# One level of Strassen's product in the up projection of a convolutional feed-forward, with all gated tiles through DRAM

## The chip, the core and the metric

The kernel runs on one core of a Trainium2 chip. The metric is the device time of one execution in microseconds (us). TensorE (PE) multiplies, with its weight loads shown apart as PEld; VectorE (DVE), ScalarE (ACT) and GpSimd (POOL) do the elementwise work; SyncE (SP) issues the DMAs of this kernel.

## The reference, cut to what matters

One layer of an encoder over 1024 prompt frames and 8 x 16 sample frames, 1152 tokens in all, D_MODEL = 1024 and D_FF = 2816. Attention, a state-space layer and the output projection come first and are the same before and after the change. Then:

```python
def conv_ffn(x, prev, w_up, conv_w, conv_b, w_down):
    up = x @ w_up                                   # [tokens, 2 * D_FF]
    up_p = jnp.concatenate([prev, up], axis=1)      # two earlier rows
    c = sum(up_p[:, j:j + L] * conv_w[j] for j in range(CONV_W)) + conv_b
    gate, val = jnp.split(c, 2, axis=-1)
    return (jax.nn.silu(gate) * val) @ w_down, up_p[:, -(CONV_W - 1):]
...
    f, new_conv = conv_ffn(rmsnorm(x, lw['norm2']), conv_prev, ...)
    x = x + f                                       # then a final rmsnorm
```

## The kernel before

Every product runs in float32r with each operand split into a high and a low part, so `mm3` (L60 to L63) issues three matmuls for one: high by high, high by low, low by high. Tokens are cut into 9 tiles of 128 (8 of the prompt, 1 of the sample).

`wout_s(t)` finishes the output projection of tile t: two halves of 512 columns, 12 matmuls each, into `po`; DVE adds the residual; the rows go to `x2_d` in DRAM; ACT squares them, `rstd` makes the norm on DVE in small pieces, ACT scales the rows. `h2_T(t)` (L1210 to L1213) transposes the scaled rows on PE into `h2T`, ACT copies them into `h2h` and DVE subtracts into `h2l`, 128x512 at a time.

The up projection runs over 22 pairs j, each of one tile of 128 gate features (i = 0) and one of 128 value features (i = 1). `load_up(j, i)` brings 8 blocks of `w_up` and splits them with the norm's gain into `uh` and `ul` (8 ACT and 8 DVE instructions of 128x128). For each of three token blocks of 384, `up_mm` runs 8 x 3 matmuls into a bank `pu`; `up_out` copies the bank to `ext` on ACT. So a pair has 2 x 3 x 8 x 3 = 144 matmuls of 384 columns.

`up_pair_end(j)` then does the convolution over time of both tiles (`up_conv`: one Identity on ACT, L1301, and two DVE instructions, L1302 and L1303, all 128x1168), Silu on ACT (L1308) and the product on DVE. POOL fills the two leading columns of `ext` (L1292, L1293) and saves the last rows (L1299, L1300). Of the gated tiles `g`, the first five (KEEP) stay in SBUF; the other 17 go to `g_d` in DRAM and are reloaded as `gr` (L1346) for the down projection.

The down projection runs over two token halves (5 and 4 tiles) by two halves of 512 output columns; for each it goes over k = 0 to 21, with `down_k` splitting a piece of `w_down` (`wd` into `wdh`, `wdl`) and of the gated tile (into `gh`, `gl`), and 3 matmuls of 512 columns per token tile into `acc`. The pool `dwA` that holds these pieces is opened ahead of the up projection, so that the first pieces are there when it ends. `conv_out` writes the saved convolution rows (`cvo`, `cvr`) while the down projection runs.

The order of the work on each engine is set by a scheduler that replays the program on its own timeline; within an engine the order is then fixed, and engines wait for each other on semaphores.

## Time and profile before

| | us |
|---|---|
| three timed runs | 1271.71, 1274.02, 1273.22 (median 1273.22) |
| profiled execution, its span | 1272.3 |
| first transposes of `h2_T` | 395.9 |
| last matmul of the up projection | about 988 |
| up projection on PE, 3168 matmuls | 549 |
| from there to the end of the span | 284 |

The span runs from the first to the last instruction of the profiled execution; the page gives no other time for it, so the median of the timed runs, 0.9 us above the span, stands beside it. A line of the page's groups names the line of the code, the engine, what is written and read, the tile and the count, then the busy time in us, the mean in ns of one, and the idle time ahead of it with what ended it.

### The profile page before, as it was taken

To read this page: it belongs to the slowest core of one execution; us is meant where nothing else is said; L and a number is where in the kernel's file an instruction comes from. 1 tells how busy PE (TensorE), PEld (TensorE's weight loads), DVE (VectorE), ACT (ScalarE), POOL (GpSimd) and SP (SyncE) were. 2 spreads that over 40 slices of the span, in tenths; PEclk is the share of its full clock that TensorE was granted. 3 is DMA by queue.
4 is the path that set the end of the run, shared out by engine and by line. 5 is a ranking of instruction groups with operands and counts; after the bars stand their busy time and mean duration, and the time that the engine had idled before them with its cause. 6 is when DMAs were issued, how large, how long until landed. Compare 5 with 4: busy or idle time off the path is not lost.

```text
span 1272.3 us, 19276 instructions
## 1 busy us (share of the span) xinstructions
PE 1237.1 (97%) x7000; PEld 1100.7 (87%) x7000; DVE 764.9 (60%) x1990; ACT 631.1 (50%) x1463; POOL 50.6 (4%) x188
## 2 busy tenths in 40 slices
PE   8999998999989999999999999999999999999996
PEld 6777776777878899999999999999999878888885
DVE  6898778887279655454445445454543446457655
ACT  7446557652576465444443545444443334345543
POOL 0000000000000000010001000100100000000000
PEclk9999999999999999999999999999999999999998
DMA  7522247649545321111212112221210862226232
GB/s 246 108 101 98 95 118 225 204 130 222 172 134 186 107 93 50 34 51 52 70 52 87 62 61 70 71 69 53 70 55 19 353 240 82 75 75 232 91 101 82
DMA packets 129409, 142.98 MB, mean 112 GB/s; under 512 B 28282, under 2 KB 93698, under 8 KB 129282
## 3 DMA queue, kind: packets, MB, share of 16 engines
q1 hardware_dynamic: 129314, 141.75, 34.8%
q8 instruction: 55, 0.90, 0.3%
q14 instruction: 40, 0.33, 0.1%
HBM read 104.07 MB, written 38.70 MB: 112 GB/s over the span
## 4 chain that ended last, share of the span: by engine, by line
PE 81%; DVE 9%; DMA 4%; ACT 3%; issue 1%; SPq 1%; DVEq 0%; ACTq 0%
PE pu L63 15%; PE pu L62 15%; PE pu L61 15%; PE acc L62 7%; PE acc L63 7%; PE acc L61 7%; PE po L61 2%; PE po L62 2%; PE po L63 2%; PE sc L66 1%; DMA scr<-in_state_conv_dram 1%; DVE tb L81 1%; DMA xr<-in_x_prompt_dram 1%; PE pos L66 1%; PE pq L63 1%
## 5 line engine op out<-in xcount | busy, mean ns | idle before, releaser
L62 PE MATMUL pu<-h2l,uh 128*128 128x384 f32 x1056 | 352.8, 334 | 0.1
L61 PE MATMUL pu<-h2h,uh 128*128 128x384 f32 x1056 | 352.7, 334 | 0.2 <-ACT h2h L1212 0.2
L63 PE MATMUL pu<-h2h,ul 128*128 128x384 f32 x1056 | 352.5, 334 | 0.0
L1241 DVE SCALAR_TENSOR_TENSOR ul<-ur,g,uh 128x128 fp32r<-128x128 f32 x352 | 107.8, 351 | 213.9 <-ACT uh L1240 213.9
L61 PEld LDWEIGHTS pu<-h2h,uh 128*128 128x128 f32 x1056 | 198.0, 188 | 0.8 <-ACT h2h L1212 0.7
L62 PEld LDWEIGHTS pu<-h2l,uh 128*128 128x128 f32 x1056 | 198.2, 188 | 0.5 <-DVE h2l L86 0.4
L63 PEld LDWEIGHTS pu<-h2h,ul 128*128 128x128 f32 x1056 | 198.2, 188 | 0.0
L1240 ACT ACTIVATE uh<-ur,g 128x128 fp32r<-128x128 f32 x352 | 112.2, 394 | 137.8 <-PE pu L62 137.0
L62 PE MATMUL acc<-wdl,gh 128*128 128x512 f32 x396 | 154.5, 390 | 0.3 <-DVE wdl L86 0.2
L63 PE MATMUL acc<-wdh,gl 128*128 128x512 f32 x396 | 154.2, 389 | 0.0
L86 DVE TENSOR_TENSOR gl<-gr,gh 128x384 fp32r<-128x384 f32 (+2 forms) x102 | 54.0, 555 | 96.9 <-ACT gh L1390 96.9
L61 PE MATMUL acc<-wdh,gh 128*128 128x512 f32 x396 | 107.7, 390 | 0.2 <-ACT wdh L1376 0.2
L1390 ACT ACTIVATE gh<-gr 128x384 fp32r<-128x384 f32 (+2 forms) x102 | 49.6, 519 | 111.4 <-PE acc L62 111.4
L1272 ACT ACTIVATE ext<-pu 128x384 f32<-128x384 f32 x88 | 43.1, 495 | 92.9 <-PE pu L63 92.9
L62 PEld LDWEIGHTS acc<-wdl,gh 128*128 128x128 f32 x396 | 74.3, 188 | 16.9 <-DVE wdl L86 1.4
L63 PEld LDWEIGHTS acc<-wdh,gl 128*128 128x128 f32 x396 | 74.3, 188 | 15.4
L61 PEld LDWEIGHTS acc<-wdh,gh 128*128 128x128 f32 x396 | 74.1, 188 | 15.6 <-ACT wdh L1376 0.4
L86 DVE TENSOR_TENSOR wdl<-wd,wdh 128x512 fp32r<-128x512 f32 x88 | 60.3, 686 | 2.2 <-ACT wdh L1376 2.2
L1376 ACT ACTIVATE wdh<-wd 128x512 fp32r<-128x512 f32 x88 | 54.1, 616 | 2.4 <-DMA wd<-in_w_down_dram 2.4
L1302 DVE SCALAR_TENSOR_TENSOR g<-ext,cw,g 128x1168 f32<-128x1168 f32 x22 | 31.6, 1434 | 34.4 <-ACT g L1301 34.4
L1308 ACT ACTIVATE cg<-cg 128x1168 f32<-128x1168 f32 x22 | 26.0, 1182 | 44.5 <-DVE cg L1303 44.5
L1302 DVE SCALAR_TENSOR_TENSOR cg<-ext,cw,cg 128x1168 f32<-128x1168 f32 x22 | 31.6, 1435 | 27.2 <-ACT cg L1301 27.2
(332 smaller groups left out, 2034.3 us busy)
## 6 DMA issues: line engine op xcount, KB each, us to landing
ur<-in_w_up_dram SPq DMA_DIRECT2D x44, 512.0 KB, 3.8
wd<-in_w_down_dram SPq DMA_DIRECT2D x88, 256.0 KB, 2.7
g_d<-g SPq DMA_DIRECT2D x17, 584.0 KB, 3.3
gr<-g_d SPq DMA_DIRECT2D x17, 584.0 KB, 10.0
...
```

The costliest lines, as they stand in the source:

```text
L61: mm(out, lh, rh, start=first, stop=False, skip_group_check=True)
L62: mm(out, lh, rl, start=False, stop=False, skip_group_check=True)
L63: return mm(out, ll, rh, start=False, stop=last, skip_group_check=True)
L66: mm(out, l, r, start=first, stop=last, skip_group_check=True)
L86: V_.tensor_tensor(o, a, b, op=op)
L1240: act(hi[:, k], raw[:, k], AF.Copy, scale=g)
L1241: stt(lo[:, k], raw[:, k], g, f(hi[:, k]), op0=OP.mult, op1=OP.subtract)
L1272: act(ext[:, 2 + nb * NBK:2 + (nb + 1) * NBK], ps, AF.Copy)
L1302: stt(o, ext[:, 1:1 + GLEN], cw[:, 1, ft:ft + 1], o, op0=OP.mult, op1=OP.add)
L1308: act(cg, cg, AF.Silu)
L1376: act(wh_, raw, AF.Copy)
L1390: act(oh_, src, AF.Copy)
```

## The change

Tokens of each tile are cut into a first and a second half of 64, and the 1024 inputs into two halves of 512. A pair j of gate and value tiles by two token halves is then a product of 2 x 2 blocks, and one level of Strassen's method (in Winograd's form) forms it with seven half products instead of eight. The pieces:

- The right operands are the blocks B11, B21, B22 of the normed input and four differences T1 to T4. `h2_T` builds them from PSUM: for each of two column pieces (kw = 2) four DVE multiplications with the norm's gain (128x128), four subtractions on POOL (`gsub`), one ACT copy of all seven (128x896) into `HH` and one DVE subtraction (128x896) into `HL`. Tiles 0 to 4 form token group 0 (320 columns per operand), tiles 5 to 8 group 1 (256 columns). Group 1's rows are read back from `x2_d`, scaled on ACT (`hr`), and go through `h2_T` between and after group 0's products of the first pair.
- The left operands are the blocks A11, A12, A22 of `w_up` and four sums S1 to S4, made on POOL (four 128x512 per pair). `prep(n)` splits one operand by one ACT and one DVE instruction of 128x512, seven products ahead.
- Each product is 2 groups x 4 blocks x 3 = 24 matmuls; a pair has 7 x 24 = 168, half of 320 columns and half of 256. Banks a, b and c collect partial sums: a bank is read out between products and then accumulated further. `collect` reads by ACT copies or by DVE additions into `ext`.
- All 22 gated tiles go to `g_d` and are reloaded. `dwA` and the pools of the reloaded tiles are opened after the up projection, since the operands take their memory; WDB is 5 instead of 6. The temporary of the convolution, `cg`, has one buffer instead of two.

```diff
+    PROD = (("A11", B11, "a", True), ("A12", B21, "b", True), ("S2", T2, "a", False), ("S1", T1, "c", True),
+            ("S3", T3, "a", False), ("A22", T4, "a", False), ("S4", B22, "c", False))
...
+        for k0 in range(0, 4, kw):
+            ks = slice(k0, k0 + kw)
+            st = pl.tile([P, 7, kw, HB], F32, name=f"st{t}_{k0}", tag="st", bufs=1)
+            b12 = pl.tile([P, kw, HB], F32, name=f"b12{t}_{k0}", tag="b12", bufs=1)
+            for o, j, c in ((st[:, B11], 0, 0), (b12, 0, 1), (st[:, B22], 1, 1), (st[:, B21], 1, 0)):
+                tt(o, pts[j][:, ks, c * HB:(c + 1) * HB],
+                   g2[:, 4 * j + k0:4 * j + k0 + kw, None].to_broadcast([P, kw, HB]), OP.mult)
+            gsub(st[:, T1], b12, st[:, B11])
+            gsub(st[:, T2], st[:, B22], st[:, T1])
+            gsub(st[:, T3], st[:, B22], b12)
+            gsub(st[:, T4], st[:, B21], st[:, T2])
+            act(HH[g][:, :, ks, tk], st, AF.Copy)
+            tt(HL[g][:, :, ks, tk], st, f(HH[g][:, :, ks, tk]), OP.subtract)
+
+    def gsub(o, a, b, op=OP.subtract):
+        nc.gpsimd.tensor_tensor(o, a, b, op=op)
...
+        if i == 0:
+            a, b = RAW[j, 0], RAW[j, 1]
+            S = {x: upW.tile([P, 4, P], F32, name=f"{x}_{j}", tag="sum", bufs=3) for x in ("S1", "S2", "S4")}
+            gsub(S["S1"], b[:, 0], b[:, 1], OP.add)
+            gsub(S["S2"], S["S1"], a[:, 0])
+            gsub(S["S4"], a[:, 1], S["S2"])
...
+        op = upW.tile([P, 2, 4, P], F32R, name=f"op{n}", tag="op", bufs=7)
+        act(op[:, 0], src, AF.Copy)
+        tt(op[:, 1], src, f(op[:, 0]), OP.subtract)
...
+    def product(n, g, pl=None):
+        j, i = divmod(n, 7)
+        _, b, bank, opens = PROD[i]
...
+        for k in range(4):
+            mm3(ps, op[:, 0, k], op[:, 1, k], HH[g][:, b, k], HL[g][:, b, k], opens and k == 0, k == 3)
...
+        if i in (0, 2, 4, 5):
+            for o, ps in quarter(j, *((0, 0), None, (0, 1), None, (1, 1), (1, 0))[i], g, a):
+                act(o, ps, AF.Copy)
+        for k, q, ps in ((1, (0, 0), b), (4, (1, 1), c), (6, (0, 1), c)):
+            if i == k:
+                for o, p_ in quarter(j, *q, g, ps):
+                    tt(o, p_, o, OP.add)
...
     for j in range(1, NF):
-        for i in range(2):
...
-            for nb in range(3):
-                up_out(j, i, nb, up_mm(j, i, nb, pup, "up"))
...
+        for i in range(7):
+            n = 7 * j + i
+            for g in range(2):
+                product(n, g)
+                collect(n, g)
+            prep(n + 7)
+            if i == 2:
                 up_pair_end(j - 1)
```

The order moves at three places. The first is PE where the up projection begins. In these names `pu00c` is bank c of pair 0 and group 0, `h2T` are transposes (by tile and half), `hh_1` is `HH` of group 1. After the change the transposes of tiles 6, 7 and 8 stand one behind the other between group 0's last product and group 1's first:

```order
L63 MATMUL pu00c<-hh_0_4791,op_5529 128x320
L1232 MATMUL h2T_0_5546<-ident,hr_5459 128x128 x4
L1232 MATMUL h2T_1_5551<-ident,hr_5459 128x128 x4
L1232 MATMUL h2T_0_5593<-ident,hr_5462 128x128 x4
L1232 MATMUL h2T_1_5598<-ident,hr_5462 128x128 x4
L1232 MATMUL h2T_0_5640<-ident,hr_5465 128x128 x4
L1232 MATMUL h2T_1_5645<-ident,hr_5465 128x128 x4
L61 MATMUL pu01a<-hh_1_5447,op_4799 128x256
L61 MATMUL pu01b<-hh_1_5447,op_4802 128x256
```

Before, the transposes of the last tile stand alone among matmuls on the first eight tiles (`pu_5492` takes blocks of tokens that are already there):

```order
L62 MATMUL pu_5492<-h2l,uh_4808 128x384
L63 MATMUL pu_5492<-h2h,ul_4809 128x384
L1210 MATMUL h2T_0_5517<-ident,h_8_5383 128x128 x4
L1210 MATMUL h2T_1_5524<-ident,h_8_5383 128x128 x4
L61 MATMUL pu_5531<-h2h,uh_4788 128x384
L61 MATMUL pu_5556<-h2h,uh_4808 128x384
L62 MATMUL pu_5531<-h2l,uh_4788 128x384
```

The transposes moved from between matmuls that could run without them to a row in which the next matmuls read what they feed.

The second is DVE at the same place, the operand build of tile 6. `st` and `b` (the program's `b12`) have one buffer each, and the row that writes the next piece waits for the row that reads this one:

```order
L86 TENSOR_TENSOR st_0_5556<-h2T_0_5546,g_4432 128x128 [waits DVE_49,PE_49]
L86 TENSOR_TENSOR b_0_5557<-h2T_0_5546,g_4432 128x128
L86 TENSOR_TENSOR st_0_5556<-h2T_1_5551,g_4432 128x128 [waits PE_49]
L86 TENSOR_TENSOR st_0_5556<-h2T_1_5551,g_4432 128x128
L86 TENSOR_TENSOR hl_1_5448<-st_0_5556,hh_1_5447 128x7x2x64 [waits Activation_49]
L86 TENSOR_TENSOR st_2_5568<-h2T_0_5546,g_4432 128x128 [waits DVE_49]
L86 TENSOR_TENSOR b_2_5569<-h2T_0_5546,g_4432 128x128
L86 TENSOR_TENSOR st_2_5568<-h2T_1_5551,g_4432 128x128 x2
L86 TENSOR_TENSOR hl_1_5448<-st_2_5568,hh_1_5447 128x7x2x64 [waits Activation_49]
```

What was one DVE subtraction for each half of a tile is now five DVE instructions for each piece, in one chain with POOL and ACT.

The third is the end of the up projection. On ACT, after the change, the convolution of the last pair (`g_11058`, `cg_11051`, then its Silu) stands ahead of the first split of `w_down`:

```order
L1349 ACTIVATE ext_10838<-pu211a 128x3x64
L1349 ACTIVATE ext_10838<-pu211a 128x4x16
L1377 ACTIVATE g_11058<-ext_10838,cw 128x1168
L1377 ACTIVATE cg_11051<-ext_10835,cw 128x1168
L1484 ACTIVATE gh_11113<-gr_11080 128x640
L1384 ACTIVATE cg_11051<-cg_11051 128x1168
L1484 ACTIVATE gh_11140<-gr_11082 128x640
L1470 ACTIVATE wdh_11109<-wd_11107 128x512
L1470 ACTIVATE wdh_11136<-wd_11134 128x512
L1470 ACTIVATE wdh_11163<-wd_11161 128x512
```

Before, the two first pieces of `w_down` had been split long ahead, and only one Identity stood between the last read-out and the first gated tile:

```order
L1274 ACTIVATE ext_10127<-pu_10182 128x256
L1275 ACTIVATE ext_10127<-pu_10182 128x8x16
L1301 ACTIVATE g_10216<-ext_10127,cw 128x1168
L1390 ACTIVATE gh_10317<-g_6180 128x640
L1376 ACTIVATE wdh_10313<-wd_10311 128x512
L1390 ACTIVATE gh_10344<-g_6398 128x640
```

On SP, after the change, the store of the last gated tile and four other DMAs stand ahead of the third reloaded tile, `gr_11105` (the first two are issued earlier):

```order
L1493 DMA x_5_12425<-x_d 128x1024
L1388 DMA g_d<-g_11058 128x1168
L1467 DMA wd_11242<-in_w_down_dram 128x512
L1467 DMA wd_11269<-in_w_down_dram 128x512
L1461 DMA out_dram<-cvr_0_11350 88x128
L1461 DMA out_dram<-cvr_0_11355 128x128
L1440 DMA gr_11105<-g_d 128x1168
L1440 DMA gr_11132<-g_d 128x1168
```

Before, the reloads follow the last store at once, and the first one is needed only for k = 5:

```order
L1237 DMA ur_10012<-in_w_up_dram 128x8x128
L1317 DMA g_d<-g_9900 128x1168
L1317 DMA g_d<-g_10119 128x1168
L1346 DMA gr_10230<-g_d 128x1168
L1346 DMA gr_10232<-g_d 128x1168
L1346 DMA gr_10255<-g_d 128x1168
```

What moved is the start of the down projection: its first pieces and its first reloads now stand behind the last pair's convolution.

More of the change, by code (lines that the diff above doesn't have):

```diff
@@ new lines, in emit, with prep @@
+    SUMS = {}
+    def prep(n):
+        j, i = divmod(n, 7)
+        if j >= NF:
+            return
+        if i == 0:
[4 more added lines that the diff above has]
+            gsub(S["S4"], a[:, 1], S["S2"])
+            SUMS[j] = dict(S, A11=a[:, 0], A12=a[:, 1], A22=b[:, 1])
+        if i == 4:
+            s3 = upW.tile([P, 4, P], F32, name=f"S3_{j}", tag="sum", bufs=3)
+            gsub(s3, RAW[j, 0][:, 0], RAW[j, 1][:, 0])
+            SUMS[j]["S3"] = s3
+        src = SUMS[j][PROD[i][0]]
+        op = upW.tile([P, 2, 4, P], F32R, name=f"op{n}", tag="op", bufs=7)
+        act(op[:, 0], src, AF.Copy)
+        tt(op[:, 1], src, f(op[:, 0]), OP.subtract)
+        OPS[n] = op
@@ L1246, in emit @@
+    load_up(0)
+    hA = h2s.enter_context(pool("hA"))
+    h_tiles(0, hA)
+    for n in range(5):
+        prep(n)
     resid(0)
@@ new lines, in quarter, with collect @@
+    def quarter(j, i, half, g, ps):
+        ext, es = EX[j, i]
+        t0, t1 = TG[g]
+        tp = min(t1, NPT)
+        v = [(ext[:, 2:2 + SEQ].rearrange("p (t h c) -> p h t c", h=2, c=HB)[:, half, t0:tp],
+              ps[:, 0:(tp - t0) * HB].rearrange("p (t c) -> p t c", c=HB))]
+        if t1 > NPT:
+            v.append((es[:, 4 * half:4 * half + 4, 2:],
+                      ps[:, (tp - t0) * HB:].rearrange("p (b s) -> p b s", s=NS)))
+        return v
+    def collect(n, g):
+        j, i = divmod(n, 7)
+        a, b, c = (BK.get((j, g, x)) for x in "abc")
+        if i in (0, 2, 4, 5):
[5 more added lines that the diff above has]
+                    tt(o, p_, o, OP.add)
@@ L1305, in up_pair_end @@
     def up_pair_end(j):
-        cg = upw.tile([P, GLEN], F32, name=f"cg{j}", tag="cg")
+        cg = upw.tile([P, GLEN], F32, name=f"cg{j}", tag="cg", bufs=1)
         up_conv(j, 0, cg)
         act(cg, cg, AF.Silu)
-        if j < KEEP:
-            g = gpool.tile([P, GLEN], F32, name=f"g{j}")
-        else:
-            g = upw.tile([P, GLEN], F32, name=f"g{j}", tag="gs")
+        g = upw.tile([P, GLEN], F32, name=f"g{j}", tag="gs")
         up_conv(j, 1, g)
         tt(g, g, cg, OP.mult)
-        GT[j] = g
-        if j >= KEEP:
-            nc.sync.dma_start(g_d[j], g)
-    for i in range(2):
-        up_begin(0, i)
-    for (j, i, nb), ps in first:
-        up_out(j, i, nb, ps)
-    load_up(1, 0)
+        nc.sync.dma_start(g_d[j], g)
+    hrs = ExitStack()
+    hrow = hrs.enter_context(pool("hrow", side="right"))
+    for t in range(*TG[1]):
+        x = hrow.tile([P, DM], F32, name=f"hr{t}", tag="hr", bufs=2)
+        nc.sync.dma_start(x, x2_d[t * P:(t + 1) * P])
+        act(x, x, AF.Copy, scale=rs2[:, t:t + 1])
+        H2[t] = x
+    load_up(1)
+    up_begin(0)
+    pl0 = {"a": (psc, "sc"), "b": (pat, "at"), "c": (pmm, "mm")}
+    for i in range(7):
+        if i + 5 < 7:
+            prep(i + 5)
+        product(i, 0, pl0)
+        collect(i, 0)
+        if i < TG[1][1] - TG[1][0]:
+            h2_T(TG[1][0] + i, hrow, 2)
+    hrs.close()
+    upw = fu.enter_context(pool("upw", 2, side="right"))
+    for i in range(7):
+        product(i, 1, pl0)
+        collect(i, 1)
+        prep(7 + i)
     ps1.close()
@@ L1406, in emit @@
                 if half == 0 and dh == 0:
-                    reload(KEEP + 2 + k)
+                    reload(2 + k)
                 gh_, gl_, wh_, wl_ = down_k(half, dh, k, nt, dwA, 2)
```

145 lines of the change are left out of this document (72 added, 73 removed).

## The prediction

> **What bounds the kernel now.** I read the busy shares first, then the chain that ended last, then busy time by stage, then the spacing of single matmuls. The profiled execution's span is 1272.3 us, 0.9 below the median of the runs (1273.22); sums are made against the span and the 0.9 is added at the end.
>
> ```profile
> span 1272.3 us, 19276 instructions
> PE 1237.1 (97%) x7000; PEld 1100.7 (87%) x7000; DVE 764.9 (60%) x1990; ACT 631.1 (50%) x1463; POOL 50.6 (4%) x188
> PE 81%; DVE 9%; DMA 4%; ACT 3%; issue 1%; SPq 1%; DVEq 0%; ACTq 0%
> 395.00:455.00 60.00, 60.00 (x325) 52.59 (x323) 41.53 (x149) 30.69 (x51) 0.69 (x6) 1.00 0.39 138
> 480.00:985.00 505.00, 505.00 (x2916) 505.00 (x2915) 239.48 (x407) 227.73 (x529) 45.11 (x158) 1.00 0.18 58
> 985.00:1140.00 155.00, 153.16 (x681) 126.41 (x680) 74.74 (x119) 60.92 (x106) 0.38 (x2) 1.00 0.46 168
> ```
>
> A window row gives PE, PEld, DVE, ACT and POOL, then granted clock, DMA share and GB/s. In the up projection PE is busy for all of 505.00 us at clock 1.00, with DVE and ACT at less than half: each matmul removed there is time, until another engine is in the way. PE is also full before it, and nearly so after. PE's durations overlap, so a matmul's cost is its spacing:
>
> ```profile
> 599.80 0.33 PE L61 MATMUL pu<-h2h,uh 128*128 128x384 f32 x1
> ...
> 603.96 0.33 PE L61 MATMUL pu<-h2h,uh 128*128 128x384 f32 x1
> 164.34 0.28 PE L61 MATMUL pkv<-wh_kv,hh 128*128 128x256 f32 x1
> ...
> 166.38 0.28 PE L61 MATMUL pkv<-wh_kv,hh 128*128 128x256 f32 x1
> 998.97 1.13 PE acc L61 x5
> 1002.37 1.13 PE acc L61 x5
> ```
>
> 384 columns: 24 steps in 4.16 us, 173.3 ns. 256 columns: 18 steps in 2.04, 113.3. 512 columns: 15 in 3.40, 226.7. The trace has no 320; halfway between 256 and 384 is 143.3 (140 with the slope from 512 to 256 laid through 256, 146.7 with the same slope laid down from 384).
>
> **Steady gain.** Before, 144 x 173.3 = 24.96 us per pair; after, 84 x (143.3 + 113.3) = 21.56. Over 22 pairs 549.1 becomes 474.3: **74.8 us less** (68.6 to 80.9 with the bounds).
>
> **Do the helpers keep up?** Their rows:
>
> ```profile
> L86 DVE TENSOR_TENSOR wdl<-wd,wdh 128x512 fp32r<-128x512 f32 x88 | 60.3, 686 | 2.2 <-ACT wdh L1376 2.2
> L1376 ACT ACTIVATE wdh<-wd 128x512 fp32r<-128x512 f32 x88 | 54.1, 616 | 2.4 <-DMA wd<-in_w_down_dram 2.4
> L1303 DVE SCALAR_TENSOR_TENSOR g<-ext,cw,g 128x1168 f32<-128x1168 f32 x22 | 31.6, 1435 | 0.8
> L86 DVE TENSOR_TENSOR g<-g,cg 128x1168 f32<-128x1168 f32 x22 | 30.2, 1375 | 0.8
> L1301 ACT ACTIVATE g<-ext,cw 128x1168 f32<-128x1168 f32 x22 | 29.9, 1360 | 0.2
> L86 DVE TENSOR_TENSOR gl<-gr,gh 128x640 fp32r<-128x640 f32 x34 | 28.1, 825 | 66.8 <-ACT gh L1390 66.8
> L1308 ACT ACTIVATE cg<-cg 128x1168 f32<-128x1168 f32 x22 | 26.0, 1182 | 44.5 <-DVE cg L1303 44.5
> L1390 ACT ACTIVATE gh<-gr 128x640 fp32r<-128x640 f32 x34 | 25.2, 740 | 74.2 <-PE acc L62 74.2
> L1274 ACT ACTIVATE ext<-pu 128x256 f32<-128x256 f32 x44 | 16.1, 366 | 11.0 <-PE pu L63 11.0
> L1275 ACT ACTIVATE ext<-pu 128x128 f32<-128x128 f32 x44 | 11.7, 265 | 0.0
> L86 DVE TENSOR_TENSOR B<-B,S__2548 128x1024 f32<-128x1024 f32 x8 | 9.7, 1216 | 0.0
> L86 DVE TENSOR_TENSOR gl<-gr,gh 128x128 fp32r<-128x128 f32 x34 | 9.7, 284 | 0.0
> L1300 POOL COPY cvt<-ext 128x16 f32<-128x16 f32 x44 | 9.6, 218 | 0.0
> L1199 ACT ACTIVATE h<-xo 128x1024 f32<-128x1024 f32 x9 | 9.5, 1059 | 0.9 <-DVE xo L773 0.9
> L1299 POOL COPY cvt<-ext 128x2 f32<-128x2 f32 x44 | 8.4, 191 | 276.7 <-ACT ext L1274 276.7
> ```
>
> ACT per pair: seven splits at 0.616, four read-outs in pieces of 320, 192 and 64 columns (0.43 + 0.32 + 0.21 on the line through 265 and 366), two Identities, a Silu: 4.3 + 3.8 + 2.7 + 1.2 = 12.1 of 21.56 us. DVE: seven splits at 0.686, three additions in the same pieces (0.48 + 0.35 + 0.22), four steps of the convolution, one product: 4.8 + 3.2 + 5.7 + 1.4 = 15.1. POOL has no two-input row. Its two copies give 1.9 ns per element on 0.19 us, so 0.43 for 128 and 1.18 for 512 with one input. Bounds for two inputs: DVE's rows below (0.28 and 0.69), twice POOL's slope above (0.68 and 2.16). I take **0.45 and 1.25**, nearest to POOL's own rows: four sums and the small copies make 6.2 us per pair. No engine comes near 21.56 alone. Laying these durations into the order of one pair, I find no wait of PE: operands are split seven products ahead, and group 1's matmuls (1.36 us) cover the read-out of group 0's bank. The least margin is about 3 us, before A22, whose read-out needs an `ext` buffer that the previous convolution must leave.
>
> A rule of the Trainium skill ("GPSIMD Engine Reference", section 3.1: about 2.6 cycles per element for two inputs at 1.2 GHz) gives an estimate of 1.1 us for 512 columns and 0.28 for 128, without dispatch; with the 0.19 us beside the elements that POOL's copies show, the sum stays, and with nothing beside them it would be 7 us lower. No row here shows a two-input instruction on POOL, so whether the trace agrees is open.
>
> **The start.** Here the change adds a chain.
>
> ```profile
> 395.89 1.04 PE L1210 MATMUL h2T<-ident,h 128*128 128x128 f32 x8
> 388.16 0.40 PE L61 MATMUL po<-oh,sh 128*128 128x512 f32 x1
> ...
> 390.73 0.40 PE L63 MATMUL po<-oh,sl 128*128 128x512 f32 x1
> 569.58 1.44 DVE L1303 SCALAR_TENSOR_TENSOR g<-ext,cw,g 128x1168 f32<-128x1168 f32 x1
> 571.16 0.10 POOL L1292 MEMSET ext<- 128x2 f32 x1 [5.53 <-DVE g L1303]
> ```
>
> One piece (half a tile) of the operand build: two DVE products (0.57), four POOL subtractions (4 x 0.45 = 1.8), hand-overs of some 0.35 together (DVE to POOL takes 0.14 in the rows: an end at 571.02, a start at 571.16), ACT on 896 columns (0.96, between 740 for 640 and 1059 for 1024), DVE on 896 (1.09, between 825 and 1216). That is 4.8 us, and as `st` has one buffer, pieces follow each other: 9.6 us per tile, with POOL's bounds 8.2 to 11.4. PE needs 24 x 0.234 = 5.6 for a tile of `po`, so PE gets ahead.
>
> From the first transposes at 395.9 come 151 `po` matmuls, 12 of 384 columns and four further transposes: tile 4 is transposed at 438.5, built at 448.1. PE had done 18 matmuls of its first piece; 18 more (2.6), S2 (1.7 and a read-out of 0.7), transposes of tile 5: 454.2. S3, A22 and S4 of group 0 run beside its build. Then nothing is left for PE: four tiles at 9.6 end at 492.6, and the first products of group 1 need them all. The rest of pair 0 (18 matmuls of 256 and four products with a read-out ahead of each, 2.0 + 8.2) ends at 502.8. Before, 22 pairs end at
>
> ```profile
> 988.44 0.39 ACT L1274 ACTIVATE ext<-pu 128x256 f32<-128x256 f32 x1 [3.67 <-PE pu L63]
> 991.61 0.74 ACT L1390 ACTIVATE gh<-g 128x640 fp32r<-128x640 f32 x1 [1.17 <-PE acc L62]
> ```
>
> 988.2, so they fill 439.1 onwards, and at the new rate pair 0 would have ended at 460.7. **The start gives back 42 us** (ten pieces on the path: 34 to 52). That the group 1 rows are read again and scaled costs nothing: 9.6 us per tile of cover for a scaling of about 1.1; without it 1.1 per tile.
>
> **The end.** `acc` followed `pu` at once before. After, once the last product ends, DVE has two additions (0.25 + 0.57), two steps for `g`, two for `cg` (5.7), then ACT has Silu, a split of the gated tile and one of `wd` (1.18 + 0.74 + 0.62): PE waits 9.1 us, then some 0.5 for the low part. The third reload stands behind the last store, two `wd` loads that wait for the splits, and two output stores; it issues about 12.5 us after the end, and lands at 16 to 17 (584 KB; `g_d` stores of that size land in 3.3):
>
> ```profile
> g_d<-g SPq DMA_DIRECT2D x17, 584.0 KB, 3.3
> gr<-g_d SPq DMA_DIRECT2D x17, 584.0 KB, 10.0
> ```
>
> Two k of 3.4 us have then been done since 9.6, and its split takes 1.6: about 1.8 more. If each reload took 10.0, 5 more. **11.4 us**, 8 to 17. Later reloads come in a burst ahead of need, at 3.4 us per k.
>
> **Sum.** 502.8 + 21 x 21.56 = 955.6; end 11.4; the rest of the kernel 1272.3 - 988.2 = 284.1; span 1251.1, and with 0.9 **1252 us**.
>
> **Rivals.**
>
> *DVE and POOL shut each other out.* The trace shows one direction:
>
> ```profile
> 571.05 1.38 DVE L86 TENSOR_TENSOR g<-g,cg 128x1168 f32<-128x1168 f32 x1
> 571.20 1.29 POOL L1293 COPY ext<-stc 128x16 f32<-128x16 f32 x1
> 558.73 0.21 POOL L1293 COPY ext<-stc 128x16 f32<-128x16 f32 x1
> ```
>
> A copy of 0.21 lasts 1.29 and ends 0.06 after a DVE instruction with two inputs in SBUF. If POOL's sums hold DVE off as well, a pair's bound is DVE plus POOL: 15.1 + 1.2 + 4 x p. At p = 1.25 that is 21.3, just under 21.56, which eats the margin. It binds from p = 1.32, and costs the whole gain (21 x 1.05 = 22 us) from p = 1.58. At 2.16 the pair takes 24.9: 1252 + 70 = **1322**. For it: the row; DVE is the fullest helper. Against: POOL's slope is measured at 1.9 with one input, and 3.2 us of DVE's work reads PSUM. Chance 0.21, nearly all of it slower.
>
> By a rule of the Trainium skill ("SBUF — State Buffer", Who interferes with whom) a DVE instruction with two SBUF inputs and a GpSimd instruction that reads SBUF lock each other out for a whole instruction, whoever starts first. The trace agrees where DVE was first (1.29 against 0.21); with POOL first no row here shows it.
>
> *Small waits in every pair.* A read-out queued behind an Identity or Silu on ACT (1.36, 1.18) comes 0.5 to 1 us late for the next product of that bank. At 0.3 to 0.9 per pair 1258 to **1271**; POOL's upper bound in the start alone adds 9. Against it speaks the margin of the walk. Chance 0.18.
>
> *A shorter start.* POOL at DVE's speed makes a piece 4.1 us and 320 columns 140 ns: 1252 - 7 - 6 = **1239**. Chance 0.1.
>
> *The narrow matmuls don't get cheaper*, bound by weight loads at the 173 ns of 384: 168 x 173.3 = 29.1 per pair, 1400. The 113 ns rows speak against it: PE and PEld have 7000 instructions each, so those matmuls too had a weight load each. Chance 0.01.
>
> **How the numbers follow.** The forecast (1240 to 1262) has 0.5. Below 1234 I leave 0.05, above 1290 some 0.13 (most of the first rival): **1234 to 1290**. A measurement of this kernel tells about 0.2%, or 2.5 us, from no change. Faster: 0.5 + 0.1 + 0.13 of the small waits + 0.02 of the first rival (p just over 1.32), 0.75; same: 0.03 of the small waits and 0.02 of the first rival; slower: the remaining 0.17 of the first rival, 0.02 of the small waits and the 0.01 of the narrow matmuls, 0.20.
>
> **What would show it.** Right: PE spacing 143 and 113 in the up projection, PE busy all of a window from 520 to 940; a gap of about 28 us in PE's `pu` ahead of group 1's first product, ended by `hl` of DVE; 9 us ahead of the first `acc`, ended by `wdh`. Wrong: POOL's 128x512 above 1.4; DVE instructions longer while POOL runs and PE waiting for `op` or for read-outs in each pair; a build piece far from 4.8 us; a reload that ends PE's idle time beyond k = 2.

## The result, and the profile after

| | before | after |
|---|---|---|
| median of the timed runs, us | 1272.47 (4 runs) | 1286.12 (1283.96 to 1289.82, 4 runs) |
| ratio of after to before | | 1.011 [1.0090, 1.0131] |
| span of the profiled execution, us | 1272.3 | 1284.0 |

The change makes the kernel slower by 1.1%. I had forecast 1252 us, 1.7% faster. The up projection did become shorter per pair, but by less than forecast, and its start and its end gave back more than that.

The page of after, with the span, PE's busy time, instructions and the shares of the chain that ended last:

```profile
span 1284.0 us, 20613 instructions
PE 1196.7 (93%) x7528; PEld 1054.0 (82%) x7528; DVE 880.3 (69%) x2062; ACT 631.3 (49%) x1353; POOL 257.5 (20%) x348
PE 69%; DVE 13%; DMA 9%; ACT 4%; issue 2%; SPq 2%; POOL 1%; DVEq 0%; ACTq 0%; POOLq 0%
```

PE has 40 us less work than before (1237.1) and the span is 12 longer: PE now waits. In the chain, DVE and DMA rise from 9% and 4% to 13% and 9%. Busy time by stage says where (columns as in the prediction: PE, PEld, DVE, ACT, POOL, then clock, DMA share, GB/s):

```profile
380.00:440.00 60.00, 50.31 (x230) 41.80 (x229) 51.54 (x159) 29.31 (x48) 20.95 (x31) 0.89 0.45 144
460.00:480.00 20.00, 11.88 (x82) 11.16 (x81) 8.59 (x23) 8.64 (x11) 5.37 (x13) 0.91 0.16 53
480.00:500.00 20.00, 7.03 (x29) 5.96 (x30) 8.03 (x21) 3.80 (x4) 8.37 (x20) 0.50 0.00 1
520.00:620.00 100.00, 100.00 (x752) 100.00 (x751) 72.55 (x95) 49.27 (x100) 45.85 (x55) 1.00 0.24 78
980.00:1000.00 20.00, 6.21 (x29) 5.19 (x28) 11.37 (x14) 6.86 (x9) 1.70 (x3) 0.62 0.91 349
```

PE is full at clock 1.00 in the steady pairs, empty for long stretches between 460 and 500 and again after 980, and already no longer full between 380 and 440, where it was full before. PE's waits from 380 to 1010 (total, times, longest):

```profile
PE h2T L1232 <- DVE b L86: 14.7, 2, 7.4
PE acc L61 <- ACT wdh L1470: 13.8, 1, 13.8
PE pu01a L61 <- ACT hh L1245: 5.9, 2, 5.6
PE po L61 <- DVE xs L1213: 4.8, 2, 4.6
PE h2T L1232 <- ACT h L1220: 4.4, 1, 4.4
PE pu00a L61 <- ACT hh L1245: 4.0, 1, 4.0
```

The first and third are the build of group 1, as forecast. The second is the end, 13.8 us where 9.1 had been forecast. The fourth and fifth lie in the output projection, where I had forecast none. The sixth, ahead of the first product of all, is the build of tile 4, the last of group 0.

PE in the steady pairs (`pu40c` is bank c, pair 4, group 0; `pu20b` and `pu210b` open bank b in pairs 2 and 21):

```profile
537.18 0.31 PE L61 MATMUL pu20b<-hh,op 128*128 128x320 f32 x1
...
599.74 0.31 PE L61 MATMUL pu40c<-hh,op 128*128 128x320 f32 x1
...
601.51 0.28 PE L61 MATMUL pu41c<-hh,op 128*128 128x256 f32 x1
...
602.94 0.28 PE L61 MATMUL pu51a<-hh,op 128*128 128x256 f32 x1
...
962.78 0.31 PE L61 MATMUL pu210b<-hh,op 128*128 128x320 f32 x1
```

19 pairs take 962.78 - 537.18 = 425.60, so **22.40 us per pair** (forecast 21.56; before 24.96). Twelve matmuls of 320 columns take 1.77 us, 147 ns each (forecast 143.3), twelve of 256 take 1.43, 119 each (113.3).

From these rows the whole difference follows. Pair 0 ends at 511.6, where the first product of pair 1 starts. With nothing in its way it would have ended at 439.1 + 22.40 = 461.5.

| term, us | forecast | measured | how measured |
|---|---|---|---|
| 22 pairs shorter | -74.8 | -56.3 | 22 x (24.96 - 22.40) |
| start | +42 | +50.1 | 511.6 - 461.5 |
| end | +11.4 | +17.8 | last product to the end of the span: 301.9, before 284.1 |
| sum | -21 | +11.6 | spans: 1284.0 - 1272.3 = 11.7 |

### The profile page after: what moved, and what is told of

Read it like the earlier page. It is cut to its first block, busy times and chain, and to the rows that moved or that the text cites. A ratio compares the mean times of both kernels' runs of the same rounds, so it can differ in the third digit from the quotient of the medians.

```text
span 1284.0 us, 20613 instructions
## 1 busy us (share of the span) xinstructions
PE 1196.7 (93%) x7528; PEld 1054.0 (82%) x7528; DVE 880.3 (69%) x2062; ACT 631.3 (49%) x1353; POOL 257.5 (20%) x348
## 4 chain that ended last, share of the span: by engine, by line
PE 69%; DVE 13%; DMA 9%; ACT 4%; issue 2%; SPq 2%; POOL 1%; DVEq 0%; ACTq 0%; POOLq 0%
PE acc L61 6%; PE acc L62 6%; PE acc L63 6%; DMA gr<-g_d 2%; DMA wd<-in_w_down_dram 2%; PE po L61 1%; DVE hl L86 1%; PE po L62 1%; PE po L63 1%; PE sc L66 1%; DMA x<-in_x_prompt_dram 1%; DVE tb L81 1%; DMA scr<-in_state_conv_dram 1%; POOL st L1249 1%; DMA xr<-in_x_prompt_dram 1%
## 5 line engine op out<-in xcount | busy, mean ns | idle before, releaser
L86 DVE TENSOR_TENSOR gl<-gr,gh 128x640 fp32r<-128x640 f32 (+2 forms) x132 | 70.1, 555 | 112.6 <-ACT gh L1484 111.1
L1484 ACT ACTIVATE gh<-gr 128x640 fp32r<-128x640 f32 (+2 forms) x132 | 64.5, 519 | 136.4 <-PE acc L62 125.6
L86 DVE TENSOR_TENSOR op<-ur,op 128x512 fp32r<-128x512 f32 x66 | 58.5, 888 | 80.2 <-ACT op L1300 80.2
L61 PEld LDWEIGHTS acc<-wdh,gh 128*128 128x128 f32 x396 | 74.6, 189 | 33.9 <-ACT wdh L1470 17.6
L86 DVE TENSOR_TENSOR op<-S,op 128x512 fp32r<-128x512 f32 x88 | 68.7, 781 | 15.6 <-ACT op L1300 12.6
L1300 ACT ACTIVATE op<-S 128x512 fp32r<-128x512 f32 x88 | 55.6, 633 | 44.1 <-PE pu161c L63 2.2
L1300 ACT ACTIVATE op<-ur 128x512 fp32r<-128x512 f32 x66 | 41.5, 631 | 31.2 <-PE pu11b L63 2.2
L86 DVE TENSOR_TENSOR g<-g,cg 128x1168 f32<-128x1168 f32 x22 | 47.7, 2170 | 9.0 <-ACT cg L1384 9.0
L1249 POOL TENSOR_TENSOR S<-ur 128x512 f32<-128x512 f32 x22 | 33.7, 1531 | 92.1 <-DMA ur<-in_w_up_dram 62.2
L1249 POOL TENSOR_TENSOR S<-ur,S 128x512 f32<-128x512 f32 x22 | 51.4, 2338 | 0.0
L1376 POOL COPY cvt<-ext 128x16 f32<-128x16 f32 x44 | 37.3, 848 | 32.3 <-ACT ext L1349 32.2
```

What stands on the lines that cost most here:

```text
L61: mm(out, lh, rh, start=first, stop=False, skip_group_check=True)
L86: V_.tensor_tensor(o, a, b, op=op)
L1249: nc.gpsimd.tensor_tensor(o, a, b, op=op)
L1300: act(op[:, 0], src, AF.Copy)
L1376: nc.gpsimd.tensor_copy(cvt[:, 2:, ft].rearrange("p (b j) -> p b j", j=2), es[:, :, NS:])
L1484: act(oh_, src, AF.Copy)
```

## The experiments

Every time is compared with runs of the kernel before on the same chip (medians 1272.1 to 1273.0). All edits are made to the kernel after, whose own interval is 1.0090 to 1.0131. The intervals of e1, e2, e5, e6 and e7 overlap it, so their gains of one or two us in the median are not clear of noise; what these runs show is where things stand in the trace of one execution.

### e1_sums_dve: POOL's sums of A on DVE

```diff
-            gsub(S["S1"], b[:, 0], b[:, 1], OP.add)
+            tt(S["S1"], b[:, 0], b[:, 1], OP.add)
...
-            gsub(s3, RAW[j, 0][:, 0], RAW[j, 1][:, 0])
+            tt(s3, RAW[j, 0][:, 0], RAW[j, 1][:, 0], OP.subtract)
```

> The four operand sums of a pair (S1 to S4, 128x512) run on DVE instead of POOL; nothing else changes. Theory A (in the steady pairs PE alone sets the time, and POOL's sums cost only where they lock DVE's small instructions of the norm while the output projection still runs): a pair stays at 22.40 us, DVE's splits go back from 0.78 and 0.89 to 0.69 us, the two idle stretches of PE near 411 to 422 us (4.4 and 4.6) shrink, the kernel gets 4 to 9 us faster. Theory B (the lock between DVE and POOL is what lifted a pair from the forecast 21.56 to 22.40): a pair falls to about 21.6 and the kernel gains 17 us more, over 20 in all.

Measured: 1284.38 us (1281.58 to 1290.06), ratio 1.0102 [1.0069, 1.0135]. Bank b opens at 532.83 in pair 2 and 958.43 in pair 21: 22.40 per pair again. From the first transposes to group 1's first product it takes 101.1 us instead of 103.2. So POOL's sums are not what makes a pair 22.40, though they and DVE do hold each other off there. PE's idle times in the output projection, which theory A had shrink, did not: with the sums in DVE's own queue PE waits 4.1 us for `h` and 6.8 behind `xs`, in three waits. The groups of the kernel after, by form (mean ns before the last bar):

```profile
L86 DVE TENSOR_TENSOR op<-S,op 128x512 fp32r<-128x512 f32 x88 | 68.7, 781 | 15.6 <-ACT op L1300 12.6
L86 DVE TENSOR_TENSOR op<-ur,op 128x512 fp32r<-128x512 f32 x66 | 58.5, 888 | 80.2 <-ACT op L1300 80.2
L86 DVE TENSOR_TENSOR g<-g,cg 128x1168 f32<-128x1168 f32 x22 | 47.7, 2170 | 9.0 <-ACT cg L1384 9.0
L86 DVE TENSOR_TENSOR wdl<-wd,wdh 128x512 fp32r<-128x512 f32 x88 | 60.5, 687 | 6.6 <-ACT wdh L1470 6.5
```

A split of 128x512 on DVE averages 781 and 888 ns in the up projection and 687 in the down projection, where POOL is idle; `g` times `cg` averages 2170 instead of 1375 before. In e1, with POOL's sums gone, the same three average 690, 683 and 1369. POOL's sums go the same way:

```profile
L1249 POOL TENSOR_TENSOR S<-ur,S 128x512 f32<-128x512 f32 x22 | 51.4, 2338 | 0.0
L1249 POOL TENSOR_TENSOR S<-S,ur 128x512 f32<-128x512 f32 x22 | 28.9, 1314 | 0.8
```

A sum of the same size averages 1314 in one place of the pair and 2338 in another, where it meets DVE instructions. By the Trainium skill ("SBUF — State Buffer", Who interferes with whom) the engine that starts first holds the shared port for its whole instruction. The rows of both engines in time, under e10 below, agree with POOL first, which the trace of before could not show. PE paid nothing for it in the steady pairs.

### e4_pe_alone: the up projection with its helpers idle

```diff
     for j in range(1, NF):
-        load_up(j + 1)
-        up_begin(j)
         for i in range(7):
...
+            OPS[7 * j + i] = OPS[7 + i]
             for g in range(2):
-                product(n, g)
-                collect(n, g)
-            prep(n + 7)
+                product(7 * j + i, g)
```

> Leaves out, for pairs 1 to 21, the splits, sums, read-outs and the convolution: the matmuls run on pair 1's operands, and pair 0's gated tile is stored for all. It measures the spacing of the matmuls with DVE, ACT and POOL idle. If the spacing is PE's own, it stays at 0.120 us for 256 columns and 0.147 for 320, and a pair at 22.40. If the other engines' traffic is what lifted it, 256 columns fall to 0.113 and a pair towards 21.56. Its whole time is not compared.

Measured (one run): 1299.82 us, which is not compared, since work is left out. From 600 to 940 us DVE, ACT and POOL have no instruction at all, and PE is busy for all 340.00 us. The spacing of single matmuls is the result; PE of this run in pair 9:

```profile
699.73 0.31 PE L61 MATMUL pu90a<-hh,op 128*128 128x320 f32 x1
...
701.49 0.28 PE L61 MATMUL pu91a<-hh,op 128*128 128x256 f32 x1
...
702.92 0.31 PE L61 MATMUL pu90c<-hh,op 128*128 128x320 f32 x1
```

1.76 us for twelve of 320 and 1.43 for twelve of 256, as with the helpers at work. 22.40 per pair is PE's own pace.

### e2_small_pieces: build pieces of one block, two buffers

```diff
-            st = pl.tile([P, 7, kw, HB], F32, name=f"st{t}_{k0}", tag="st", bufs=1)
-            b12 = pl.tile([P, kw, HB], F32, name=f"b12{t}_{k0}", tag="b12", bufs=1)
+            st = pl.tile([P, 7, kw, HB], F32, name=f"st{t}_{k0}", tag="st", bufs=2)
+            b12 = pl.tile([P, kw, HB], F32, name=f"b12{t}_{k0}", tag="b12", bufs=2)
...
-            h2_T(t - 1, sgp, 2)
+            h2_T(t - 1, sgp, 1)
...
-            h2_T(TG[1][0] + i, hrow, 2)
+            h2_T(TG[1][0] + i, hrow, 1)
```

> The operands of h2_T are built in four pieces of one column block instead of two pieces of two, with two buffers each (the same memory). Theory A (the build at 9.3 us per tile is latency: one piece waits for the whole chain of the one before): pieces overlap, a tile takes 5 to 6 us, group 1's first product starts 12 to 18 us earlier, the kernel gets 12 to 20 us faster. Rival (DVE and POOL shut each other out, so that the build is bound by their sum): about 7.7 us per tile, 4 to 8 us faster. If smaller pieces only add fixed parts: no gain.

Measured: 1283.72 us (1282.17 to 1288.10), ratio 1.0096 [1.0069, 1.0124]. In group 1 the transposes come at 480.22, 487.74 and 494.81, 7.1 to 7.5 us apart instead of 9.24: the pieces overlap, but a tile still costs about as much as POOL's sixteen subtractions (0.32 us each) and DVE's four with both inputs in SBUF (0.63 each) laid end to end, 7.6. That is the rival's price, and fits the two shutting each other out. Group 0 lost most of what group 1 won: from the first transposes to the first product it takes 64.6 us instead of 61.2, with one wait of 8.5 us for the norm (`h`, L1220). Counted from the first transposes, pair 0 ends only 0.9 us earlier (117.2 instead of 118.1).

### e6_small_group1: the same in group 1 alone

```diff
-            st = pl.tile([P, 7, kw, HB], F32, name=f"st{t}_{k0}", tag="st", bufs=1)
+            st = pl.tile([P, 7, kw, HB], F32, name=f"st{t}_{k0}", tag="st", bufs=1 + int(t >= TG[0][1]))
...
-            h2_T(TG[1][0] + i, hrow, 2)
+            h2_T(TG[1][0] + i, hrow, 1)
```

> Only group 1's operands are built in small pieces with two buffers; group 0 stays as in the changed kernel. Run e2 took 7.3 us per tile in group 1 instead of 9.2, but lost time in group 0, where DVE is shared with the norm. Theory A: group 1's first product comes 4 to 6 us earlier and the kernel gets 3 to 6 us faster. Rival (the chain's gain is lost again because all four tiles' rows must first be read and scaled): 0 to 1 us.

Measured: 1284.71 us (1282.65 to 1286.75), ratio 1.0096 [1.0079, 1.0113]. From group 0's first product to group 1's first it takes 39.2 us instead of 41.95, a gain of 2.8 where 4 to 6 were expected, and from the first transposes to the end of pair 0 115.9 instead of 118.1.

### e5_late_prep: pair 0's splits and sums behind the output projection

```diff
-    for n in range(5):
-        prep(n)
     resid(0)
...
+        if t == 7:
+            with tc.issue_after(LS_[7].ins):
+                for n in range(5):
+                    prep(n)
```

`LS_[7]` is the last residual addition of tile 7.

> Pair 0's first five operands are prepared behind the eighth tile of the output projection instead of ahead of the first; all else as in the changed kernel. Theory A (in the output projection DVE is full: its splits of pair 0, 0.69 us each, and the waits behind POOL's sums stand ahead of the norm's small instructions and of the read-outs that PE waits for): the idle stretches of 4.4 and 4.6 us near 411 to 422 us and the half clock behind them go to under 3 us together, tile 4 is transposed 4 to 8 us earlier, the kernel gets 3 to 8 us faster. Rival (the operand build of tiles 0 to 3 alone fills DVE): the idle time only moves, 0 to 2 us.

Measured: 1284.41 us (1282.18 to 1284.85), ratio 1.0090 [1.0071, 1.0108]. Tile 4 is transposed at 439.9 instead of 449.6. Counted from the first transposes that is 47.6 us instead of 56.2 (forecast 42.6). But counted in the same way the first product gains only 1.1 us (60.1 instead of 61.2), and the first of group 1 0.6 (102.6 instead of 103.2). PE's waits from 380 to 560 in this run:

```profile
PE pu00a L61 <- ACT hh L1247: 6.2, 2, 5.8
PE po L61 <- DVE xs L1215: 4.4, 1, 4.4
PE h2T L1234 <- ACT h L1222: 2.3, 1, 2.3
```

The wait for the norm (`h`) fell from 4.4 to 2.3, and the one for the first operand grew from 4.0 to 5.8. PE reaches the chain earlier, and the chain of splits and builds on DVE ends little earlier: the idle time mostly moves.

### e3_late_loads: residual rows issued behind the reloads

```diff
-            nc.sync.dma_start(GT[j], g_d[j])
+            RL[j] = nc.sync.dma_start(GT[j], g_d[j])
...
-    nc.sync.dma_start(fgb, bcast_row(final_g, DM))
...
+                    with tc.issue_after(RL[9].ins):
+                        nc.sync.dma_start(fgb, bcast_row(final_g, DM))
+                        for u in range(t0, t0 + nt):
+                            nc.sync.dma_start(X3[u], x2_d[u * P:(u + 1) * P])
```

> The loads of the final norm's gain and of the five residual tiles (3 MB), which now stand ahead of the down projection's first loads on SP, are issued behind the reload of the tenth gated tile. Theory A (the first split of w_down waited for a load that stood behind them): PE's idle time ahead of the first acc falls from 13.8 to 6 to 9 us and the kernel gets 5 to 9 us faster. Rival (the idle time is the convolution's chain on DVE and ACT, about 9 us, and the half clock after it): 0 to 4 us faster, idle above 11.

Measured: 1289.19 us (1288.75 to 1291.10), ratio 1.0133 [1.0109, 1.0156]. Not faster than the kernel after, and in the median 3 us slower, which neither theory had (the intervals overlap a little). The wait ahead of the first `acc` shrank as hoped, and others came; PE from 980 to 1060 in this run:

```profile
PE acc L61 <- ACT wdh L1471: 9.8, 4, 3.7
PE acc L61 <- ACT gh L1485: 2.5, 1, 2.5
PE acc L62 <- DVE wdl L86: 1.3, 1, 1.3
```

13.6 us of waiting in sum, in six pieces up to 1044, against 17.0 in the kernel after, of which 13.8 stand in one piece. But some of the pieces cost clock as well:

```profile
1003.78 0.54 PE L61 MATMUL acc<-wdh,gh 128*128 128x512 f32 x1 [2.50 <-ACT gh L1485]
1004.12 0.63 PE L62 MATMUL acc<-wdl,gh 128*128 128x512 f32 x1
...
1007.53 0.39 PE L62 MATMUL acc<-wdl,gh 128*128 128x512 f32 x1
```

After 2.50 us of idle time the spacing is 0.43 for 3.4 us (eight steps in 3.41), then 0.227 again. SP's queue tells why the later waits come: nine reloads, of 584 KB each, go out in 4.71 us from 998.60, and the pieces of `w_down` that PE needs next stand behind them. What e7 and e9 change in the order of that queue shows whether it is this.

### e7_reload_order: w_down kept one step behind the reloads

```diff
-        nc.sync.dma_start(raw, w_down[0, k * P:(k + 1) * P, dc])
+        with tc.issue_after(RL[min(k + 1, NF - 1)].ins) if half == 0 and dh == 0 and k >= WDB else ExitStack():
+            nc.sync.dma_start(raw, w_down[0, k * P:(k + 1) * P, dc])
...
+                if half == 0 and dh == 0 and k == NF - 3:
+                    with tc.issue_after(RL[NF - 1].ins):
```

The residual rows and the saved convolution rows go behind the last and the eleventh reload.

> Run e3 started the down projection 10 us earlier and lost more than that within the next 60 us, where reloads stood behind loads that wait for buffers, and behind the residual tiles. Here the gain and the residual tiles are issued behind the last reload, loads of w_down from the sixth on behind the reloads of their k, and the saved convolution rows later. Theory A (the end's cost is the order of the loads on SP): first acc about 4 us after the last product, PE idle below 4 us after that, 6 to 11 us faster than the changed kernel. Rival (the first 50 us of the down projection are bound by the bytes: 12.8 MB of reloads at some 390 GB/s are 33 us and as much again for the rest): PE idle moves to later waits for gh, 0 to 4 us faster.

Measured: 1286.15 us (1285.28 to 1287.73), ratio 1.0109 [1.0093, 1.0124]. The 6 to 11 us of theory A did not come. Waits of 3.75, 2.4 and 1.1 near the start, one of 1.1 at 1026, and one of 4.5 at 1034: reloads still run ahead as far as their buffers allow and starve a `w_down` piece later. From the last product to the last `acc` 290.3 us, against 292.2 in the kernel after.

### e9_paced_loads: reloads paced by w_down too

```diff
-                    reload(2 + k)
+                    with tc.issue_after(WL[0, 0, k - 2].ins) if k >= 6 else ExitStack():
+                        reload(2 + k)
```

On top of e7: the reload of tile k + 2 goes out behind the load of `w_down` for k - 2 (`WL`).

> As e7, and in addition the reload of gated tile k + 2 is issued behind the load of w_down of step k - 2, so that the two streams alternate on SP. In e7 the first acc came 10 us earlier, but waits of 4.5 and 1.1 us for the split of w_down came some 40 us later, behind a burst of seven reloads, each long wait with a stretch of half clock. Theory A (order on the queue): those waits go, 4 to 9 us faster than e7, 1277 to 1282. Rival (bytes): PE's idle time in the first 60 us stays at 9 us or more, within 2 us of e7.

Measured: 1277.63 us (1274.23 to 1279.83, 6 runs), ratio 1.0032 [1.0018, 1.0047]: 8.5 us less than the kernel after, as theory A had it. The edit touches the order of SP's queue alone; the scheduler's order on ACT changed with it, as the part on the end says. PE's waits of over 1 us between 960 and 1060:

```profile
986.12 1.47 PE L61 MATMUL acc<-wdh,gh 128*128 128x512 f32 x5 [3.75 <-ACT wdh L1472]
990.53 0.80 PE L62 MATMUL acc<-wdl,gh 128*128 128x512 f32 x1 [2.31 <-DVE wdl L86]
999.57 0.50 PE L61 MATMUL acc<-wdh,gh 128*128 128x512 f32 x1 [1.13 <-ACT gh L1486]
```

7.2 us, and none of that size later. From the last product to the last `acc` 281.3 us; before the change it was 274.1, with the first `acc` right behind the last product.

### e8_together: e5, e6 and e7 in one

```diff
+            with tc.issue_after(LS_[7].ins):
...
+            st = pl.tile([P, 7, kw, HB], F32, name=f"st{t}_{k0}", tag="st", bufs=1 + int(t >= TG[0][1]))
...
+        with tc.issue_after(RL[min(k + 1, NF - 1)].ins) if half == 0 and dh == 0 and k >= WDB else ExitStack():
```

> The edits of e5, e6 and e7 in one kernel. If they are independent as theory A has it (start and end are separate places), the gains add: 12 to 22 us faster than the changed kernel, 1264 to 1274, at or below the kernel before. If the start is bound by DVE's sum of work, less than 8.

Measured: 1279.00 us (1277.75 to 1279.97), ratio 1.0052 [1.0038, 1.0065], 7.1 us less than the kernel after where 12 to 22 were expected. From the first transposes to the end of pair 0 it takes 112.9 us instead of 118.1: the late splits and the small pieces gain 5.2 together, where alone they gained 0.6 and 2.2. The end kept later waits, as in e7.

### e11_e8_paced: e8 with the paced loads of e9

```diff
+            with tc.issue_after(LS_[7].ins):
...
+                    with tc.issue_after(WL[0, 0, k - 2].ins) if k >= 6 else ExitStack():
+                        reload(2 + k)
```

> The start of e8 (late preparation, small pieces in group 1, sums on POOL) with the paced loads of e9. In e10 the sums on DVE shortened the norm's chain but stood ahead of the last operand pieces and made a new wait of 5.2 us. Theory A (start and end are separate, so gains add): e8 less the 10 us that the down projection lost in e8 against e9 from the last product to the last acc (291.4 against 281.3): 1267 to 1271, 2 to 6 us faster than the kernel before. If the loads' pacing depends on the start: 1274 or more.

Measured: **1270.22 us (1267.44 to 1275.20, 12 runs), ratio 0.9981 [0.9968, 0.9994]**, the only version whose whole interval lies below the kernel before, by 0.2%. From this run's windows:

```profile
440.00:460.00 20.00, 13.97 (x64) 12.00 (x63) 15.95 (x50) 6.61 (x11) 11.59 (x18) 0.83 0.47 158
460.00:480.00 20.00, 10.38 (x68) 9.49 (x66) 10.49 (x46) 8.72 (x14) 9.23 (x32) 0.83 0.16 53
480.00:500.00 20.00, 10.47 (x59) 9.29 (x60) 11.19 (x42) 7.54 (x16) 9.42 (x33) 0.66 0.00 1
```

PE still stands idle for 25 of these 60 us. Pair 0 ends at 504.8, 43 us later than with a full PE. That is most of what keeps this form of the product from its 56 us; the end keeps some 8 more (291.8 us from the last product to the end of the span, before 284.1).

### e10_start_and_end and e12_sums_pinned: POOL's sums out of the norm's way

e10 puts pair 0's four sums on DVE, on top of e11's edits; e12 leaves them on POOL and issues them behind tile 1's build (`GS[1]`).

```diff
+            sb = gsub if j else tt
+            sb(S["S1"], b[:, 0], b[:, 1], OP.add)
```

```diff
+            with tc.issue_after(LS_[7].ins), tc.issue_after(GS[1].ins):
+                for n in range(5):
+                    prep(n)
```

> The start edits of e5 and e6, pair 0's four sums on DVE instead of POOL (behind the eighth tile), and the loads as in e9. Theory A (POOL's long sums lock DVE's one-column instructions of the norm, three of which took 1.0 to 1.2 us instead of 0.15 in e8, and PE waits for the read-out behind them): the waits near 412 and 419 us fall from 6.7 together to under 4, and with the end of e9 the kernel is 6 to 11 us faster than e8, 1268 to 1273: level with the kernel before. Rival (DVE's sum of work there): the start stays as in e8 and only e9's gain shows.

> As e11, with pair 0's sums still on POOL but issued behind the operand build of tile 1, so that they do not run beside the norm of the second token block. Theory A (the lock by POOL's long sums is what stretched three one-column instructions of that norm to 1.0 to 1.2 us): no DVE instruction of one or three columns above 0.6 us between 411 and 418 us, the wait of the read-out near 419 us falls from 4.4 to under 3, 1 to 3 us faster than e11. Rival (DVE's queue alone makes that wait): within 1 us of e11.

The reason for both is in the kernel after, DVE and POOL in time (start, duration):

```profile
413.07 1.62 POOL L1249 TENSOR_TENSOR S<-ur 128x512 f32<-128x512 f32 x1 [3.21 <-DMA ur<-in_w_up_dram]
...
419.26 1.65 POOL L1249 TENSOR_TENSOR S<-ur,ur 128x512 f32<-128x512 f32 x1 [0.76 <-DVE rsb L86]
```

```profile
413.68 1.02 DVE L86 TENSOR_TENSOR rs<-rsb,rst 128x1 f32<-128x1 f32 x1
...
418.02 0.15 DVE L86 TENSOR_TENSOR rs<-rsb,rst 128x1 f32<-128x1 f32 x1
...
419.71 1.21 DVE L86 TENSOR_TENSOR rst<-rsb 128x3 f32<-128x3 f32 x1
```

A product of one column takes 0.15 us where no sum of 512 columns runs beside it. Beside such a sum, a small instruction ends with POOL's (413.68 + 1.02 = 414.70 against 414.69; 419.71 + 1.21 = 420.92 against 420.91). The norm is a chain of such small instructions, and the residual addition that PE waits for stands behind it.

Measured: e10 1274.41 us (1270.35 to 1278.34, 12 runs), ratio 1.0009 [0.9997, 1.0021]; e12 1271.53 (1269.35 to 1277.86, 12 runs), ratio 0.9989 [0.9975, 1.0002]. In e10 PE's wait behind `xs` ahead of `po` fell from 4.3 in e11 to 3.4, but a new wait of 5.2 for an operand came at 460.40 (DVE had the sums to do as well), and pair 0 ended 117.6 us behind the first transposes, against 112.7 in e11. In e12 three of the four sums still ran from 413.20 to 417.17, beside the norm, and three of its small rows still took 1.1 to 1.3 (the longest is two instructions); the wait was 5.2, and pair 0 ended 115.2 us behind the first transposes. In the whole time e12 is not to be told from e11. That the lock lengthens the norm is shown by the rows. In e10, with no sum on POOL there, no small instruction of this norm between 411 and 417 us takes over 0.43, and its last one starts 23.2 us behind the first transposes, against 25.8 in e11. But the residual addition then waits 1.61 us for a load of its row (`xs` from `xa_d`). So of the 2.6 us by which the lock lengthened the norm, PE got back 0.9 in that wait, and in e10 lost more at the operand.

## Why the prediction was wrong, point by point

**What bounds the kernel**: right. PE is busy 100.00 of 100 us in the steady pairs, and DVE at 73% holds it nowhere.

**Steady gain**: right in kind, and outside its own bounds (68.6 to 80.9; measured 56.3). The step that failed is the spacing. For 320 columns I took 143.3, halfway between 113.3 and 173.3, and measured 147, my upper bound. For 256 columns I took 113.3 from one run of `pkv` matmuls and gave it no bound, and that was a favourable sample. Other `pkv` rows of the same trace of before were there to be read, PE at another place:

```profile
71.11 0.28 PE L61 MATMUL pkv<-wh_kv,hh 128*128 128x256 f32 x1
...
72.40 0.28 PE L63 MATMUL pkv<-wh_kv,hl 128*128 128x256 f32 x1
```

11 steps in 1.29, 117 ns. In the trace of after, the stage that ran at 113.3 runs at 118, though nothing in it was changed. 256, 320, 384 and 512 columns at 120, 147, 173.3 and 226.7 lie on one line, 0.417 ns per column and 13.3 beside it. Drawn through 384 and 512 alone, which were both in the prediction, it would have given 120 and 146.7 and a pair of 22.40. The line with 113.3 as an end bent away from it. 84 x (0.147 - 0.1433) + 84 x (0.1196 - 0.1133) = 0.84 per pair, 17.6 us over the 21 pairs behind pair 0: half of the miss of 32.9 between the forecast span (1251.1) and 1284.0. e4 shows that the pace is PE's; why some `pkv` rows ran at 113.3 stays open.

**Helpers**: right. POOL's 1.31 for 512 columns and 0.47 for 128, undisturbed, are close to the 1.25 and 0.45 of the forecast, and PE waits for no helper in the steady pairs. The estimate from the Trainium skill's "GPSIMD Engine Reference" (section 3.1) with the 0.19 us beside the elements, 1.3 and 0.47, agrees with these rows. The rival of the two engines shutting each other out was right in its mechanism and wrong in its price: with the waits in them POOL's four sums average 1.62, from which its formula gives 22.8 per pair, but e1, which takes the sums off POOL, and e4, which has none, both keep 22.40. Two of the signs that were to show the forecast wrong did appear, POOL's sums above 1.4 and longer DVE instructions, but they cost nothing while PE does not wait.

**Start**: forecast 42, measured 50.1. Counted from the first transposes, which came 2.5 us earlier than in the trace of before, pair 0 ends after 118.1 us where 106.9 were forecast. The build was sized well where DVE has little else to do: `hl` comes every 4.65 us in group 1 (468.65 to 501.19, eight of them; forecast 4.8), and a tile takes 9.24 (9.6). The step that failed is group 0's build, and with it "PE gets ahead". The ten pieces of tiles 0 to 4 were to be done 52.2 us after the first transposes (448.1 - 395.9), and take 66.9, 6.7 from one `hl` to the next (the last ends at 460.38):

```profile
398.91 1.08 DVE L86 TENSOR_TENSOR hl<-st,hh 128x896 fp32r<-128x896 f32 x1
...
459.29 1.09 DVE L86 TENSOR_TENSOR hl<-st,hh 128x896 fp32r<-128x896 f32 x1 [2.32 <-ACT hh L1245]
```

Tile 4 was to be transposed at 438.5, and came at 449.6. I had counted PE's own work up to there, and the builds, but not that DVE now had the builds, pair 0's splits and the norm to do in one stretch: PE waited 4.4 for `h` and 4.6 behind `xs`, and ran some of what followed at half the clock (the eight transposes at 415.94 take 1.97 instead of 1.04). From 395 to 455 DVE is busy 54.18 us of 60 and PE 46.01; before it was 41.53 and 60.00. The experiments show that tile 4's lateness by itself is not the price: e5 took 8.6 us of it away, and group 0's build still ended 66.2 us after the first transposes; only with the shorter pieces of group 1 as well (e8) did the start give 5. No run takes the norm or the splits off DVE, so that they stretch group 0's build is read from the rows, not shown by a run.

**End**: forecast 11.4, measured 17.8, just above the bound of 17. The step that failed is which wait ends last ahead of the first `acc`. I had the gated tile's chain on DVE and ACT set it, 9.1 us, with the loads of `w_down` there already. But SP issues in order, and the loads of `w_down` stand behind the final norm's gain and residual rows:

```profile
980.74 0.33 SPq L1447 DMA_DIRECT2D fgb<-in_final_g_dram  x1
981.12 0.91 SPq L1493 DMA_DIRECT2D x<-x_d  x2
982.12 1.09 SPq L1440 DMA_DIRECT2D gr<-g_d  x2
983.26 1.72 SPq L1493 DMA_DIRECT2D x<-x_d  x3
985.02 6.01 SPq L1467 DMA_DIRECT2D wd<-in_w_down_dram  x5
```

The first of them goes out at 980.74, as the last matmul on group 0's operands ends (980.40 + 0.31), which fits memory that comes free there. The first `w_down` piece is issued at 985.02, and its split starts at 995.25, after 3.53 us in which ACT has nothing but this load to wait for. The residual rows are needed only after the 22 steps of k (3.4 us each). In e3, which moves the gain and these rows back and nothing else, SP from 975 us shows:

```profile
974.99 18.03 SPq L1468 DMA_DIRECT2D wd<-in_w_down_dram  x6
```

The first of that run went out at 974.49, and in e9 at 972.90, some 9 us ahead of the last product: the memory of `w_down` was free by then, and in the kernel after its loads only stood behind others. The forecast's chain was near the mark as far as it went: ACT is through with it at 991.72, and with one split more PE would have waited about 10 us. It is no bound either, since its order was not fixed: in e3, e7 and e9 the scheduler put the first splits of `w_down` ahead of the last Silu on ACT (985.45 and 989.17 in e9), and PE waits 3.75. PE of after, from the first `acc`:

```profile
995.93 2.50 PE L61 MATMUL acc<-wdh,gh 128*128 128x512 f32 x5 [13.79 <-ACT wdh L1470]
...
1002.60 0.62 PE L61 MATMUL acc<-wdh,gh 128*128 128x512 f32 x2
```

13.8 us of idle time, and then the half clock, which the forecast had nowhere: 15 matmuls and three transposes take 6.67 us, some 3 more than at 0.227 each. e9 takes 8.5 us off the whole; e3 and e7, which have the same 3.75 ahead of the first `acc` and gain nothing, show that it takes the order of the whole stretch of loads, not of the first few.

**The sign**: the slower cases had 0.20, nearly all on the lock between DVE and POOL in the steady pairs. Slower it became, but not by that way: three terms, each off by 6 to 18 us to the same side, moved the sum from -21 to +12. The rivals of small waits in each pair, a shorter start and narrow matmuls at the old price did not come. A gain that is the small difference of two large numbers, 75 of gain against 53 given back, needed a rival in which all terms lie at their unfavourable end.

Not tried: leaving the build out, two full buffers for its pieces, the norm or the splits of pair 0 off DVE, and the differences on PE. Whether the 43 us at the start of e11 can be had is open.
